# Placing the tables, mask and rotation of the first attention pair in another pool, loading two later pairs block by block, and one result five slots later

## The chip, the cores and the metric

The kernel runs on one core of a Trainium2 chip. The metric is the device time of one execution in microseconds (us); lower is better. PE is the matrix engine, DVE the vector engine, ACT the scalar engine, POOL the GpSimd engine, SP the engine that issues most DMAs.

## The reference

One decoder layer with 512 tokens, width 2048, eight attention heads and eight retention heads of 128, all in float32:

```python
h = rms_norm(x, g_mix)
aq, ak, av, rq, rk, rv, rg = split(h @ w_in)
aq = rotate(rms_norm(aq, q_norm)); ak = rotate(rms_norm(ak, k_norm))   # per head
a_out = block-causal softmax attention(aq, ak, av)                     # 8 heads
r = retention_chunkwise(rotate(rq), rotate(rk) / sqrt(128), rv)        # 8 heads
r_out = silu(rg) * (rms_norm(r) * g_ret)
x = x + concat(a_out, r_out) @ w_o
x = x + (silu(h2 @ w_gate) * (h2 @ w_up)) @ w_down                     # h2 = rms_norm(x)
x = x + (p @ w_ple_proj) * sigmoid(rms_norm(x) @ w_ple_gate + b)
```

With 512 tokens and blocks of 256 the selection of past blocks takes every past block, so attention is plain causal attention.

## The kernel before

**Arithmetic.** Every float32 product is made of three passes. An operand is split (`split`, lines 54 and 55) into a high part, which ACT copies (`wh`, `qkH`, `PH`), and a low part, which DVE subtracts (`wl`, `qkL`, `PL`); `mm3` (line 63) then issues high by high, high by low, low by high. So each weight tile of 128x1024 costs ACT one copy and DVE one subtraction before PE can use it. Transposes go through PE with an identity (line 68, tiles `tp`).

**First stage.** `run(beside)` makes the first projections: the q and k of pair 0 (`Plain`), then four groups by a seven-product scheme: values, the q and k of pairs 1 and 2 (`pairs`), values, and the gates (`gates`, whose silu results `sg` are stored to DRAM, lines 622 and 623; the last of them are made from tiles `e1` and `e5`, printed as `e`). The q and k of pairs 0 to 2 go to DRAM as blocks `zd[i][b]` of 128 rows and are read back as `zr`. The evacuation tiles of the stage lie in a pool `ev` on the right side of SBUF. The stage ends with `ev_ctx.close()`; the pools opened after it may lie on the same bytes, and a tile that does waits until the last access to what lay there is done.

**Mixing stage.** It follows at line 671. Five projections of 32 slots each (pair 3, then four retention pairs) run on PE, and `tick()` counts slots; a slot is six matmuls of 128x512. `at_slot(n, fn)` puts the pieces of attention and retention (turn q and k, scores, softmax, transposed weights, result) between the slots. PE's instructions keep the order in which they are written (`keep_in_program_order`); the order on DVE, ACT, POOL and SP is set when the kernel is built, by a scheduler that simulates the engines. `ATTEND`, `RETAIN` and `MIXED` are the tables of slots; the last entry of a `RETAIN` row is the slot of `result` (transposes of `r`, line 1028), `MIXED[i]` that of `mixed`, which splits a pair's two results into factors, sends them to DRAM (`mix<-o`, line 217) and so precedes the reload `s<-mix` (line 243). From slot 161 on the small projection `pp` runs (line 1115), then the first products of the output projection.

**The code around the change.** `sides` (gains and mask), `cs`, `sn` and the tables `tabs` (printed as `rope`) are loaded and built at lines 751 to 779, in pool `ap`, which is the first pool on the right side. `in_place` rotates one block of `zr`: two products with the sine table into `m` (line 832), one with the cosine table (line 830), one sum (line 81); ACT then scales the k half (line 854). For pair 0 this happens at once, for pairs 1 and 2 at slots 12 to 15 and 27 to 30, behind `load_pair` at slots 6 and 24. `qk_pair` and `p_tiles` give the split q and k and the tiles `PH` and `PL` that hold transposed softmax weights; line 928 sets one strip of `PH` and `PL` to zero, once.

Of the kernel before, what the change touches and what calls it, by code (L numbers as in the profile page):

```python
# [11 lines left out]
F32R = mybir.dt.float32r  # L12
# [5 lines left out]
P = 128  # L18
T = 512
D = 2048  # L20
NB = T // P
# [12 lines left out]
def layer_kernel(ctx, tc, x, xT, pT, g_mix, wqk, w_vg, qk_norm, g_ret, w_ow, g_ffn,  # L34
                 w_gu, w_dn, g_ple, w_pl, b_pg, w_pp,
                 ident_c, rope_c, ropeT_c, decay_c, mask_c, out):
    nc = tc.nc
    PSUM = bass.MemoryType.PSUM

    def pool(name, bufs=1, side="left", **kw):  # L40
        return tc.tile_pool(name=name, bufs=bufs, side=side, reuse_waits="tile", **kw)
# [8 lines left out]

    def split(H, L, src, scale=None):

        if scale is None:
            return (nc.scalar.activation(H, src, AF.Copy),  # L54
                    nc.vector.tensor_tensor(L, src, H.bitcast(F32), op=ALU.subtract))  # L55
        return (nc.scalar.activation(H, src, AF.Copy, scale=scale),
                nc.vector.scalar_tensor_tensor(L, src, scale, H.bitcast(F32),
                                               op0=ALU.mult, op1=ALU.subtract))
# [81 lines left out]
    def paced(ins, by):  # L140
        tc.add_manual_dep(ins.ins, by.ins.name, mybir.DependencyInfo(mybir.DependencyClass.Sync, mybir.DependencyReason.DATA),
                          reason="paced")
# [17 lines left out]
    lead = [None]  # L160
# [32 lines left out]
    def factors(a0, a1, sink):  # L193
# [7 lines left out]
        for p in ORDER:  # L201
            if p in first:
                first[p]()
            H, L, end = sink(p)
            split(H, L, made[p])
            end()
# [350 lines left out]
    zd = [[dram.tile([P, T], F32, name=f"z{i}_{b}") for b in range(NB)] for i in range(3)]  # L557
# [31 lines left out]
    def values(i):  # L589
        def finish(th, nh, b, part, _):  # L590
            tb = 2 * th + b
            H = ev_tile("o", 4, name="vH", dt=F32R)
            L = ev_tile("o", 4, name="vL", dt=F32R)
            split(H, L, part, rstd[0][:, tb:tb + 1])
# [74 lines left out]


    mix_ctx = ctx.enter_context(ExitStack())
    ap = mix_ctx.enter_context(pool("ap", side="right"))
    pools["ev"] = ev2 = mix_ctx.enter_context(pool("ev_mix", side="right"))
    acc_ctx = ctx.enter_context(ExitStack())
# [9 lines left out]
    def at_slot(n, fn):  # L684
        assert n > slot[0]
        pieces.setdefault(n, []).append(fn)
# [41 lines left out]
    def raw_pair():  # L728
        return [rawq.tile([P, 2, T], F32, name="zr", tag="bd") for _ in range(2)]

    def projection(rows):

        accs = [acc_p.tile([P, T], F32, name="acc", tag="acc") for _ in range(4)]
        for u in range(NC // 2):
            wh, wl = weights()
            for f in range(4):
                tick()
                at = slice(f * P, (f + 1) * P)
                for c in range(2):
# [4 lines left out]
                    else:  # L744
# [9 lines left out]
                                    ap=[[0, P], [HD, 2], [1, HD]]))  # L754
# [5 lines left out]
    cs, sn = (ap.tile([P, NB, HD], F32, name=n, tag="pt", bufs=2) for n in ("cs", "sn"))  # L760
    nc.sync.dma_start(cs, rope_c[:, 0])
    nc.sync.dma_start(sn, rope_c[:, 1])
    def load_pair(i, by=None):
        z = raw_pair()
        for b in range(NB):
            ins = nc.sync.dma_start(z[b // 2][:, b % 2], zd[i][b])
            if by is not None:
                paced(ins, by)
        blocks[i] = [z[b // 2][:, b % 2] for b in range(NB)]
        return ins  # L770

    blocks = {}
# [4 lines left out]
            nc.vector.tensor_tensor(tabs[1][:, s, :, here], sn[:, :, here],  # L777
                                    gain[:, s:s + 1, there].to_broadcast([P, NB, 64]), op=ALU.mult)
    rstd1 = rstd[0]
    last_load = load_pair(0)  # L780
    for _ in range(4):
        fetch(last_load)

# [7 lines left out]

    def qk_pair():
        H = ap.tile([P, T], F32R, name="qkH", tag="qkH", bufs=4)
        L = ap.tile([P, T], F32R, name="qkL", tag="qkL", bufs=4)
        return H, L

    def v_of(i):
# [5 lines left out]

    def p_tiles():

        PH = ap.tile([P, 1664], F32R, name="PH", tag="PH")
        PL = ap.tile([P, 1664], F32R, name="PL", tag="PL")
        return PH, PL

    kept_p = []  # L810
# [46 lines left out]
    def in_place(i, b, made, norms):  # L857
        of = blocks[i][b]
        sq = squares(of) if i == 0 else None
        m = rm_tile("m", (P, 2, 2, 2, HD // 2))  # L860
        z = of.rearrange("p (s h d) -> p s h d", s=2, h=2)
        whole, *halves = turn(z, m, of, b)
        for step in halves + [whole]:
            step()
        norms.append(norm(b, sq) if i == 0 else known[i][b])
        made.append(rotated(z, m, norms[b]))

    def qk_attn(i):

        made, norms = [], []  # L870
        if i == 0:
            for b in range(NB):
                in_place(0, b, made, norms)
        elif i < NPAIR - 1:
            at_slot((6, 24)[i - 1], lambda: load_pair(i, lead[0]))
            for b in range(NB):
                at_slot((12, 27)[i - 1] + b, lambda b=b: in_place(i, b, made, norms))
        else:
            got, ins = [], None
            for b, acc in enumerate(projection(True)):  # L880
                z = rp_tile("z", (P, 2, 2, HD))
                m = rm_tile("m", (P, 2, 2, 2, HD // 2))
                got.append((z, m, squares(acc)))
                for step in turn(z, m, acc, b):
                    ins = step()
            with tc.issue_after(ins.ins):
                for b, (z, m, sq) in enumerate(got):
                    norms.append(norm(b, sq))
                    made.append(rotated(z, m, norms[b]))
        return made, norms  # L890
# [151 lines left out]
    def mixed(i, made):  # L1042
# [10 lines left out]
              ((73, four(77), four(81), 89), (83, four(87), four(91), 99)))  # L1053
    RETAIN = (((100, 100, 103, 109, 116), (108, 110, 111, 117, 123)),
# [3 lines left out]
    MIXED = (28, 56, 81, 104, 126, 151, 168, 191)  # L1058

    def heads(i, made):  # L1060

# [304 lines left out]
```

## Time and profile before

| | us |
|---|---|
| median of 3 runs | 2364.56 (2363.38 to 2364.84) |
| profiled execution, its own time | 2362.4 |
| its span | 2360.6 |
| PE busy | 2300.4, 97% |
| DVE busy | 1928.0, 82% |
| ACT busy | 1230.6, 52% |
| mean granted PE clock | 0.991 |

The span is the stretch from the first to the last recorded instruction; the profiled execution's own time has 1.8 us around it. Busy PE time counts matmuls as they overlap, so PE's idle stretches, and the stretches in which the granted clock is half, are what can be won without less work. In a timeline row the bracket holds the idle time of that engine just before the row and what ended it.

### The profile page before, as it was taken

To read this page: it belongs to the slowest core of one execution; us is meant where nothing else is said; L and a number is where in the kernel's file an instruction comes from. 1 tells how busy PE (TensorE), PEld (TensorE's weight loads), DVE (VectorE), ACT (ScalarE), POOL (GpSimd) and SP (SyncE) were. 2 spreads that over 40 slices of the span, in tenths; PEclk is the share of its full clock that TensorE was granted. 3 is DMA by queue.
4 is the path that set the end of the run, shared out by engine and by line. 5 is a ranking of instruction groups with operands and counts; after the bars stand their busy time and mean duration, and the time that the engine had idled before them with its cause. 6 is when DMAs were issued, how large, how long until landed. Compare 5 with 4: busy or idle time off the path is not lost.

```text
span 2360.6 us, 29420 instructions
## 1 busy us (share of the span) xinstructions
PE 2300.4 (97%) x10445; PEld 1896.0 (80%) x10445; DVE 1928.0 (82%) x2601; ACT 1230.6 (52%) x1882; POOL 116.2 (5%) x135
## 2 busy tenths in 40 slices
PE   9999995899999999999999999999999999999999
PEld 7888874788887887888888888888888878888877
DVE  8887876777767897789888988898879887888798
ACT  8645453455555566445544554455445433447644
POOL 0004010000111000000000000000000000000000
PEclk9999997999999999999999999999999999999999
DMA  7635863546676869585457645865595776769863
GB/s 243 239 124 172 267 182 100 154 155 178 217 226 250 325 231 394 155 254 193 153 176 254 205 144 177 251 206 146 194 388 200 248 312 196 274 242 351 299 206 125
DMA packets 183843, 519.72 MB, mean 220 GB/s; under 512 B 20240, under 2 KB 33168, under 8 KB 179600
## 3 DMA queue, kind: packets, MB, share of 16 engines
q1 hardware_dynamic: 169600, 467.50, 55.3%
q0 software_dynamic: 13952, 50.34, 10.1%
q8 instruction: 82, 1.34, 0.2%
q14 instruction: 65, 0.53, 0.1%
q10 hardware_dynamic: 144, 0.01, 0.0%
HBM read 413.95 MB, written 149.95 MB: 239 GB/s over the span
## 4 chain that ended last, share of the span: by engine, by line
PE 53%; DVE 4%; DMA 3%; issue 1%; ACT 0%; SPq 0%; ACTq 0%; DVEq 0%
PE Y L63 23%; PE Z L63 15%; PE X L63 14%; DVE wl L55 2%; DMA raw<-in_w_dn 2%; DVE raw L81 2%; PE tp L68 1%; ACT wh L54 0%; DMA s<-a 0%; DMA raw<-in_w_gu 0%; DMA pp<-pp 0%; DMA xin<-x 0%; DVE e L81 0%; DVE o L55 0%; DVE t L78 0%
## 5 line engine op out<-in xcount | busy, mean ns | idle before, releaser
L54 ACT ACTIVATE wh<-raw 128x1024 fp32r<-128x1024 f32 (+1 forms) x740 | 782.7, 1059 | 873.7 <-PE Y L63 304.8
L55 DVE TENSOR_TENSOR wl<-raw,wh 128x1024 fp32r<-128x1024 f32 (+1 forms) x740 | 900.2, 1219 | 293.5 <-ACT wh L54 292.0
L63 PE MATMUL Y<-wh,s 128*128 128x512 f32 (+1 forms) x1704 | 537.9, 389 | 0.8 <-ACT wh L54 0.8
L81 DVE TENSOR_TENSOR raw<-raw 128x1024 f32<-128x1024 f32 x348 | 419.4, 1218 | 25.1 <-DMA raw<-in_w_vg 10.9
L63 PE MATMUL Z<-wh,s 128*128 128x512 f32 x1212 | 382.4, 389 | 0.2 <-ACT wh L54 0.2
L63 PEld LDWEIGHTS Y<-wh,s 128*128 128x128 f32 x1704 | 319.3, 188 | 66.6 <-ACT wh L54 1.8
L63 PE MATMUL Y<-wl,s 128*128 128x512 f32 x852 | 333.3, 391 | 0.8 <-DVE wl L55 0.7
L63 PE MATMUL X<-wh,s 128*128 128x512 f32 x1008 | 319.1, 390 | 1.7 <-ACT wh L54 1.7
L63 PEld LDWEIGHTS Z<-wh,s 128*128 128x128 f32 x1212 | 227.2, 188 | 46.5 <-ACT wh L54 0.7
L63 PE MATMUL Z<-wl,s 128*128 128x512 f32 (+1 forms) x606 | 238.7, 394 | 2.9 <-DVE wl L55 2.7
L63 PEld LDWEIGHTS X<-wh,s 128*128 128x128 f32 x1008 | 189.1, 188 | 41.4 <-ACT wh L54 2.5
L63 PE MATMUL X<-wl,s 128*128 128x512 f32 x504 | 197.2, 391 | 1.2 <-DVE wl L55 1.2
L63 PEld LDWEIGHTS Y<-wl,s 128*128 128x128 f32 x852 | 160.1, 188 | 35.6 <-DVE wl L55 3.0
L63 PE MATMUL Y<-wh,r 128*128 128x512 f32 x520 | 170.9, 390 | 1.3 <-ACT wh L54 1.1
L63 PE MATMUL acc<-h,wh 128*128 128x512 f32 x512 | 162.0, 398 | 0.0
L63 PEld LDWEIGHTS Z<-wl,s 128*128 128x128 f32 x606 | 113.9, 188 | 28.6 <-DVE wl L55 5.9
L63 PE MATMUL Z<-wh,r 128*128 128x512 f32 x372 | 122.0, 389 | 0.0
L63 PEld LDWEIGHTS Y<-wh,r 128*128 128x128 f32 x520 | 97.4, 188 | 21.9 <-ACT wh L54 2.1
L63 PEld LDWEIGHTS X<-wl,s 128*128 128x128 f32 x504 | 94.7, 188 | 21.6 <-DVE wl L55 2.3
L63 PEld LDWEIGHTS acc<-h,wh 128*128 128x128 f32 x512 | 91.8, 189 | 15.4 <-DVE zr L963 0.3
L63 PE MATMUL Y<-wl,r 128*128 128x512 f32 x260 | 102.4, 394 | 0.5 <-DVE wl L55 0.5
L63 PE MATMUL acc<-h,wl 128*128 128x512 f32 x256 | 100.4, 392 | 0.0
(241 smaller groups left out, 2839.3 us busy)
## 6 DMA issues: line engine op xcount, KB each, us to landing
raw<-in_w_gu SPq DMA_DIRECT2D x172, 512.0 KB, 5.6
raw<-in_w_dn SPq DMA_DIRECT2D x85, 512.0 KB, 6.6
a<-o SPq DMA_DIRECT2D x154, 256.0 KB, 4.9
raw<-in_w_vg SPq DMA_DIRECT2D x64, 512.0 KB, 5.1
s<-a SPq DMA_DIRECT2D x21, 1536.0 KB, 8.6
raw<-in_wqk SPq DMA_DIRECT2D x47, 512.0 KB, 4.9
raw<-in_w_ow SPq DMA_DIRECT2D x32, 512.0 KB, 6.8
xin<-x SPq DMA_DIRECT2D x60, 256.0 KB, 5.9
```

Of the source, the lines that this page charges most:

```text
L54: return (nc.scalar.activation(H, src, AF.Copy), nc.vector.tensor_tensor(L, src, H.bitcast(F32), op=ALU.subtract))
L55: nc.vector.tensor_tensor(L, src, H.bitcast(F32), op=ALU.subtract))
L63: ins = nc.tensor.matmul(*args, **kw)
L68: ins = nc.tensor.transpose(o, a, ident)
L81: nc.vector.tensor_tensor(o, a, b, op=ALU.add)
```

## The change

A new pool `far` is opened before `ap` on the right side, and `qkL`, `PH` and `PL` are taken from it; the tables, `cs`, `sn`, the mask and the rest stay in `ap`, which now begins behind `far`. `load_pair` becomes `load_block`: pairs 1 and 2 (the second and third) are loaded one block at a time, at slots 5, 7, 9, 11 and 17, 19, 21, 23, and each block is rotated three slots after its load. In `RETAIN` the result of the second head of the third retention pair goes from slot 165 to 170, and `MIXED` of that pair from 168 to 171.

```diff
     mix_ctx = ctx.enter_context(ExitStack())
+    far = mix_ctx.enter_context(pool("far", side="right"))
     ap = mix_ctx.enter_context(pool("ap", side="right"))
...
-    def load_pair(i, by=None):
-        z = raw_pair()
-        for b in range(NB):
-            ins = nc.sync.dma_start(z[b // 2][:, b % 2], zd[i][b])
-            if by is not None:
-                paced(ins, by)
-        blocks[i] = [z[b // 2][:, b % 2] for b in range(NB)]
+    def load_block(i, b, by=None):
+        if b == 0:
+            z = raw_pair()
+            blocks[i] = [z[b // 2][:, b % 2] for b in range(NB)]
+        ins = nc.sync.dma_start(blocks[i][b], zd[i][b])
+        if by is not None:
+            paced(ins, by)
         return ins
...
-    last_load = load_pair(0)
+    last_load = [load_block(0, b) for b in range(NB)][-1]
...
-        L = ap.tile([P, T], F32R, name="qkL", tag="qkL", bufs=4)
+        L = far.tile([P, T], F32R, name="qkL", tag="qkL", bufs=4)
...
-        PH = ap.tile([P, 1664], F32R, name="PH", tag="PH")
-        PL = ap.tile([P, 1664], F32R, name="PL", tag="PL")
+        PH = far.tile([P, 1664], F32R, name="PH", tag="PH")
+        PL = far.tile([P, 1664], F32R, name="PL", tag="PL")
...
-            at_slot((6, 24)[i - 1], lambda: load_pair(i, lead[0]))
             for b in range(NB):
-                at_slot((12, 27)[i - 1] + b, lambda b=b: in_place(i, b, made, norms))
+                n = (5, 17)[i - 1] + 2 * b
+                at_slot(n, lambda b=b: load_block(i, b, lead[0]))
+                at_slot(n + 3, lambda b=b: in_place(i, b, made, norms))
...
-              ((142, 142, 145, 151, 158), (150, 152, 153, 159, 165)),
+              ((142, 142, 145, 151, 158), (150, 152, 153, 159, 170)),
...
-    MIXED = (28, 56, 81, 104, 126, 151, 168, 191)
+    MIXED = (28, 56, 81, 104, 126, 151, 171, 191)
```

Three places show what this does to the order in which the engines get their instructions. The first is SP at the end of the first stage; `sg` is the DRAM tensor of gate results, `raw<-in_wqk` a weight tile of the next projection. Before:

```order
L711 DMA raw_3721<-in_wqk 128x1024
L623 DMA sg_150<-e1_2616 128x512
L623 DMA sg_150<-e1_2617 128x512
L711 DMA raw_3864<-in_wqk 128x1024
L753 DMA sides_3043<-in_qk_norm 128x256
L757 DMA sides_3043<-in_mask_c 128x128
L761 DMA cs_3049<-in_rope_c 128x512
L762 DMA sn_3050<-in_rope_c 128x512
```

And now:

```order
L768 DMA zr_3063<-z0_3_189 128x512
L712 DMA raw_3068<-in_wqk 128x1024
L712 DMA raw_3072<-in_wqk 128x1024
L754 DMA sides_3046<-in_qk_norm 128x256
L758 DMA sides_3046<-in_mask_c 128x128
L762 DMA cs_3052<-in_rope_c 128x512
L763 DMA sn_3053<-in_rope_c 128x512
L802 DMA v_3178<-v_0_148 128x2x256 x4
L623 DMA sg_150<-e5_2674 128x512
```

The four table loads, and the loads of `v` behind them, stood behind the last six stores of `sg`; they now stand ahead of all six.

The second place is DVE over the same stretch; `wl` is the low part of a weight tile, `e1<-Y` the evacuation of the stage's last product. Before:

```order
L55 TENSOR_TENSOR wl_3138<-raw_3041,wh_3137 128x1024
L78 TENSOR_TENSOR e1_2616<-Y0_2958,e1_2616 128x512
L78 TENSOR_TENSOR e1_2617<-Y1_2959,e1_2617 128x512
L55 TENSOR_TENSOR wl_3142<-raw_3065,wh_3141 128x1024
L928 TENSOR_SCALAR PH_3246<-ident_72 128x128
L928 TENSOR_SCALAR PL_3247<-ident_72 128x128
L756 TENSOR_SCALAR sides_3043<-sides_3043 128x128
L774 TENSOR_TENSOR rope_3047<-cs_3049,sides_3043 128x512 x2
L777 TENSOR_TENSOR rope_3048<-sn_3050,sides_3043 128x4x64 x4
L832 TENSOR_TENSOR m_3075<-zr_3059,rope_3048 128x4x64
```

And now, where the tables and the eight products into `m` stand further ahead still:

```order
L55 TENSOR_TENSOR wl_2954<-raw_2414,wh_2953 128x1024
L831 TENSOR_TENSOR zr_3062<-zr_3062,rope_3050 128x512 x2
L831 TENSOR_TENSOR zr_3063<-zr_3063,rope_3050 128x512 x2
L55 TENSOR_TENSOR wl_2973<-raw_2437,wh_2972 128x1024
L81 TENSOR_TENSOR zr_3062<-zr_3062,m_3078 128x512
L81 TENSOR_TENSOR zr_3062<-zr_3062,m_3092 128x512
L81 TENSOR_TENSOR zr_3063<-zr_3063,m_3106 128x512
L55 TENSOR_TENSOR wl_3137<-raw_3042,wh_3136 128x1024
L81 TENSOR_TENSOR zr_3063<-zr_3063,m_3120 128x512
L55 TENSOR_TENSOR wl_3141<-raw_3044,wh_3140 128x1024
L78 TENSOR_TENSOR e1_2616<-Y0_2958,e1_2616 128x512
L78 TENSOR_TENSOR e1_2617<-Y1_2959,e1_2617 128x512
```

Tables and rotation of the first pair have moved from behind `e1<-Y` to ahead of it, between the `wl` of the stage's last products; the zero strips of `PH` and `PL` come behind the first `qkL`.

The third place is DVE where the second pair's softmax meets the third pair's rotation, in the projection of the fourth pair; `pt` is a softmax row block, `mx` its maximum, `zr` and `m` the third pair's blocks, `z` and `m` made from `acc` the fourth pair's. Before:

```order
L830 TENSOR_TENSOR zr_3582<-zr_3582,rope_3047 128x512
L832 TENSOR_TENSOR m_3791<-acc_3129,rope_3048 128x4x64 x2
L830 TENSOR_TENSOR z_3797<-acc_3130,rope_3047 128x512
L832 TENSOR_TENSOR m_3798<-acc_3130,rope_3048 128x4x64 x2
L915 TENSOR_SCALAR mx_3738<-mx_3738,ms0_3_1957 128x1
L830 TENSOR_TENSOR z_3804<-acc_3131,rope_3047 128x512
L830 TENSOR_TENSOR zr_3582<-zr_3582,rope_3047 128x512
L919 RECIPROCAL sm_3704<-sm_3704 128x1
L81 TENSOR_TENSOR zr_3582<-zr_3582,m_3746 128x512
L919 RECIPROCAL sm_3742<-sm_3742 128x1
L81 TENSOR_TENSOR zr_3582<-zr_3582,m_3759 128x512
L920 TENSOR_SCALAR pt_3703<-pt_3703,sm_3704 128x384
```

And now:

```order
L917 TENSOR_SCALAR mx_3724<-mx_3724,ms0_2_1948 128x1
L913 TENSOR_TENSOR at_3750<-at_3750,sides_3046 128x128
L55 TENSOR_TENSOR wl_3741<-raw_3738,wh_3740 128x1024
L915 TENSOR_REDUCE mx_3755<-at_3750 128x1
L55 TENSOR_TENSOR PL_3248<-tp_3745,PH_3247 128x2x128
L921 RECIPROCAL sm_3728<-sm_3728 128x1
L831 TENSOR_TENSOR z_3793<-acc_3132,rope_3050 128x512
L833 TENSOR_TENSOR m_3794<-acc_3132,rope_3051 128x4x64 x2
L917 TENSOR_SCALAR mx_3755<-mx_3755,ms0_3_1957 128x1
L922 TENSOR_SCALAR pt_3727<-pt_3727,sm_3728 128x384
```

The third pair's rotation is gone from this stretch (it now stands some 30 to 60 instructions earlier, among the softmax of the first pair's second head), and `pt` of 128x384 has one `z` and one pair of `m` ahead of it where it had three `z` and the whole rest of the rotation. On PE the order of all instructions is the same but for one place: the four transposes of `r` that begin the `result` of the seventh pair's second head stand 30 matmuls, five slots, later.

## Rows read from the trace of the kernel before

**Rows 1.** The page's first section: busy time, share of the span, instructions.

```profile
PE 2300.4 (97%) x10445; PEld 1896.0 (80%) x10445; DVE 1928.0 (82%) x2601; ACT 1230.6 (52%) x1882; POOL 116.2 (5%) x135
```

**Rows 2.** What PE waited for from 340 to 480 us: engine, line and tile, what it waited for, us in total, times, longest.

```profile
PE tp L68 <- DVE zr L81: 17.9, 1, 17.9
PE tp L68 <- DVE pt L920: 10.7, 2, 8.3
PE tp L68 <- DVE PL L55: 3.3, 1, 3.3
PE tp L68 <- DVE qkL L55: 0.9, 1, 0.9
```

**Rows 3.** The same from 690 to 760 us.

```profile
PE tp L68 <- DVE r L1022: 4.7, 2, 3.8
PE at L63 <- DVE PL L55: 1.3, 1, 1.3
```

**Rows 4.** Busy time by engine in the four stretches in which the granted clock is half (stretch, its length, busy time and instructions of PE, weight loads, DVE, ACT, POOL; granted clock; DMA share; GB/s).

```profile
362.80:383.30 20.50, 5.03 (x15) 3.47 (x15) 11.50 (x26) 2.98 (x9) 0.00 (x0) 0.50 0.42 132
407.10:410.60 3.50, 3.50 (x12) 2.80 (x11) 1.26 (x3) 1.74 (x3) 0.00 (x0) 0.51 0.00 0
451.50:461.80 10.30, 5.99 (x20) 5.14 (x21) 7.62 (x19) 5.19 (x11) 0.00 (x0) 0.50 0.06 14
707.50:714.40 6.90, 5.67 (x15) 4.46 (x16) 5.29 (x16) 3.33 (x8) 0.55 (x1) 0.51 1.03 417
```

**Rows 5.** The same columns for three other stretches.

```profile
346.56:361.10 14.54, 13.41 (x60) 10.77 (x58) 7.33 (x7) 7.51 (x9) 3.04 (x3) 1.00 0.62 214
...
420.00:430.00 10.00, 9.15 (x47) 7.45 (x47) 7.51 (x19) 4.67 (x10) 0.87 (x1) 1.00 0.41 112
...
710.00:740.00 30.00, 29.95 (x137) 24.90 (x136) 20.82 (x33) 18.82 (x40) 6.64 (x13) 0.93 1.04 377
```

**Rows 6.** SP's queue in order of time: start, time to issue, DMA, number.

```profile
335.23 6.51 SPq L711 DMA_DIRECT2D raw<-in_wqk  x3
...
361.71 0.94 SPq L623 DMA_DIRECT2D sg<-e  x2
...
363.24 0.41 SPq L753 DMA_DIRECT2D sides<-in_qk_norm  x1
...
364.64 0.42 SPq L762 DMA_DIRECT2D sn<-in_rope_c  x1
...
728.88 1.46 SPq L243 DMA_DIRECT2D s<-mix  x3
```

**Rows 7.** DVE in order of time at the end of the first stage.

```profile
359.53 1.28 DVE L78 TENSOR_TENSOR e<-Y,e 128x512 f32<-128x512 f32 x2
...
363.92 0.23 DVE L928 TENSOR_SCALAR PH<-ident 128x128 fp32r<-128x128 f32 x1 [1.60 <-DMA sg<-e]
...
367.85 0.23 DVE L756 TENSOR_SCALAR sides<-sides 128x128 f32<-128x128 f32 x1 [2.54 <-DMA sides<-in_qk_norm]
```

**Rows 8.** DVE's groups of instructions from 360 to 382 us: busy us, mean ns, idle before.

```profile
L832 DVE TENSOR_TENSOR m<-zr,rope 128x256 f32<-128x256 f32 x8 | 2.8, 416 | 0.0
L830 DVE TENSOR_TENSOR zr<-zr,rope 128x512 f32<-128x512 f32 x4 | 2.5, 680 | 0.0
L81 DVE TENSOR_TENSOR zr<-zr,m 128x512 f32<-128x512 f32 x4 | 2.5, 680 | 0.0
L777 DVE TENSOR_TENSOR rope<-sn,sides 128x256 f32<-128x256 f32 x4 | 1.4, 419 | 0.0
L774 DVE TENSOR_TENSOR rope<-cs,sides 128x512 f32<-128x512 f32 x2 | 1.3, 688 | 1.4 <-DMA cs<-in_rope_c 1.4
```

**Rows 9.** PE in order of time: the first transposes, the first matmul, two later ones three matmuls apart, and the first scores (`at`) of the mixing stage, and a matmul of the output projection.

```profile
377.89 2.28 PE L68 MATMUL tp<-ident,zr 128*128 128x128 f32 x4 [17.92 <-DVE zr L81]
379.83 0.77 PE L63 MATMUL acc<-wh,h 128*128 128x512 f32 x1
...
384.27 0.39 PE L63 MATMUL acc<-wl,h 128*128 128x512 f32 x1
...
384.96 0.39 PE L63 MATMUL acc<-wl,h 128*128 128x512 f32 x1
...
386.09 0.28 PE L63 MATMUL at<-qkH 128*128 128x256 f32 x1
...
740.67 0.40 PE L63 MATMUL X<-wh,s 128*128 128x512 f32 x1
```

**Rows 10.** DVE's groups from 445.3 to 455.4 us, in which PE waits for `pt`.

```profile
L830 DVE TENSOR_TENSOR z<-acc,rope 128x512 f32<-128x512 f32 x3 | 2.0, 678 | 0.0
L81 DVE TENSOR_TENSOR zr<-zr,m 128x512 f32<-128x512 f32 x3 | 2.0, 671 | 0.0
L832 DVE TENSOR_TENSOR m<-zr,rope 128x256 f32<-128x256 f32 x4 | 1.5, 419 | 1.0 <-DMA mix<-o 1.0
...
L830 DVE TENSOR_TENSOR zr<-zr,rope 128x512 f32<-128x512 f32 x2 | 1.4, 676 | 0.0
```

**Rows 11.** From issue to landing of DMAs: of the blocks `zr` from 360 to 440 us (least, median, most); of the tables from 355 to 400 us and of the reload from 700 to 740 us (KB each, median).

```profile
DMA to landing us min/median/max: 2.6/3.5/8.4
...
sn<-in_rope_c SPq DMA_DIRECT2D x1, 256.0 KB, 5.4
...
s<-mix SPq DMA_DIRECT2D x9, 512.0 KB, 8.9
```

## The prediction

> **What bounds the kernel now.** I read the page's busy times first. PE is busy for 97% of the span, DVE for 82%, ACT for 52% [rows 1]: PE sets the time, and less waiting, or less work at half clock, is all that an edit of order can win. Then the view of what PE waited for, over the two stretches that the change touches. From 340 to 480 us there are 32.8 us of waits, all before transposes, all for DVE: 17.9 in one piece, 10.7 in two (8.3 and 2.4), 3.3, 0.9 [rows 2]. From 690 to 760 there are 4.7 for `r` (3.8 and 0.9) and 1.3 for `PL` [rows 3]. [...]
>
> The 17.9 us are explained by two queues. SP issues the last stores of `sg` at 361.71 and the tables only behind them, `sides` at 363.24, `sn` at 364.64 [rows 6]. DVE, whose order is fixed, stands at the zero strip of `PH` until such a store is done, and then waits for `sides` until 367.85 [rows 7]. Only then come tables and rotation, 2.8 + 2.5 + 2.5 + 1.4 + 1.3 us [rows 8] and 0.23 for the gain, 10.7 us in all, and PE's first transposes begin at 377.89 [rows 9].
>
> **The change, part by part.** No instruction is added; the orders of DVE, ACT and SP change.
>
> *Tables and first rotation.* SP now issues the tables behind the second of the three weight loads of its row at 335.23 [rows 6], so about 338 to 340. With the 5.4 us that `sn` took to land [rows 11] they are there at about 345. The `v` loads and six stores of `sg` come behind them; nobody waits for these but the zero strips, which are past the first `qkL` now. The 10.7 us of DVE work come between the `wl` of the stage's last products. There DVE is busy for 7.33 of 14.54 us [rows 5], so it has 7.2 us to spare and 3.5 spill over. Queued behind is `e<-Y`, which ended at 359.53 + 1.28 = 360.8 [rows 7] and would end at 364.3. It empties the banks of the stage's last product, and the mixing stage's accumulators lie where those lay, so PE's first matmul waits for it: 364.4 in place of 379.83 [rows 9], 15.4 us. Of the 3.5 us from 379.83 to 383.3, run at half clock, 1.7 would come back, if the remaining wait of some 4 us (part of it inside the stage, before a `wl`) leaves the clock alone. I take the middle, 16.3. The ends: 20.4 (the whole wait and the whole 2.5 of half clock), and 13.0 (a third of the 7.2 us cannot be filled, and the clock stays low).
>
> On the clock the rows say this: beside the wait of 0.9 us the granted clock stays at 1.00 [rows 5], and behind 3.8 us it is at 0.51 [rows 3, 4]. [...]
>
> *Second pair by blocks, slots 5 to 14.* PE waits here 3.3 + 2.4 us and loses 1.75 to the clock. In the new order two of the four sums of that rotation stand behind the `pt` that PE waits for; that is 2 x 0.68 [rows 8], 1.4. Half of the clock's price may go with it, 0.9. I take 2.3; the ends are 0 (another instruction ends the wait) and 7.5 (all of it).
>
> *Third pair by blocks, slots 17 to 26.* Its rotation moves from 440 to 455 us to about 425, among the softmax of the first pair's second head, where PE waited only 0.9 us. Two pairs of `m` (4 x 0.42) and one `zr` (0.68) [rows 8] now stand ahead of the last `pt`, and behind that in the queue the `qkL` and `PL` that PE's next transposes need: 2.4 us lost. The ends are a gain of 0.9 and a loss of 4.7, two whole blocks at 0.84 + 0.68 + 0.68 each and a little.
>
> What it leaves is the place of the 8.3 us wait. In that stretch DVE spends 2.0 + 1.5 + 1.4 = 4.9 us on the third pair [rows 10], and the `pt` came last. Now one `z` (0.68), two `m` (0.84) and some 0.6 of small rows stand ahead of it: 2.1 us of the wait stay, 6.2 go, and with them the 3.0 of half clock, since 2.1 is nearer to the 0.9 that cost no clock than to the 8.3 that did. I take 9.2; the ends are 4.9 (the rotation's own time, no clock back) and 11.3.
>
> *The late result.* The transposes of `r` move five slots on. Three matmuls take 0.69 us at full clock (384.27 to 384.96, [rows 9]), a slot 1.38, five of them 6.9; the `r` that PE waited 3.8 us for is then there 3 us ahead. So 3.8 go, and the 2.8 of half clock: 6.6. But what comes behind is a reload. From 710 to 740 us the DMA share is 1.04 [rows 5]; the engines have nothing free. `s<-mix`, issued at 728.88 [rows 6], lands 8.9 us later [rows 11], at 737.8, and PE uses the last of it at 740.67 [rows 9]. If PE is 6.6 us earlier, it wants it at 734.1, and waits 3.7. The later 0.9 and 1.3 [rows 3] lie behind DVE work that then has time; half of them goes, 1.1. I take 6.6 - 3.7 + 1.1 = 4.0; the ends are 0 and 8.8.
>
> [...]
>
> The sum is 16.3 + 2.3 - 2.4 + 9.2 + 4.0 = 29.4 us. From the profiled execution's own 2362.4 this gives 2333.0; that execution was 2.2 under the median of the runs, so the time I forecast is 2364.6 - 29.4 = 2335. Nothing past 760 us changes its order in a way that a wait there shows.
>
> **The rivals.** *Only the first wait goes.* The later waits are DVE's, DVE has the same work in a shorter time there, and what it no longer does in one place it does in another; then the other four terms come to about nothing, and the time is 2364.6 - 15.4 = 2349. For it speaks that every wait in [rows 2] is for DVE; against it, that 4.9 us leave the stretch of the longest of them.
>
> *All goes.* Waits and half clock together: 32.8 + 4.7 + 1.3 and 10.1 us, 48.9; the time is 2316. Against it is the 3.5 us that DVE cannot fit in, and the full DMA engines at 710.
>
> *The tables land late.* Were they served only at the stage's end, at 361, the 10.7 us would follow, q and k would be ready at 372 and not at 379.7, and the first term would be 8 instead of 16.3: 2343. The share of 0.62 [rows 5] says that there is room earlier.
>
> *Slower: eight waits for blocks.* Each block's rotation now stands in DVE's queue for a load issued three slots (4.1 us) before, and the softmax of the pair in work stands behind it. The blocks landed in 2.6 to 8.4 us, 3.5 at the median [rows 11]. If all eight took 8.4, DVE would stand 4.3 us each time, 34.4 in all: 5.0 us more than the sum, 2370. It decides from a landing time of 4.1 + 29.4 / 8 = 7.8 us on every block; at the median it costs nothing.
>
> **How the numbers follow.** The forecast 0.60 (its own range 2327 to 2343), only the first wait 0.20, all 0.10, tables late 0.06, slower 0.04. The ends of all the terms add up to 13.2 and 48.9 us, that is 2351 and 2316. The range 2319 to 2351 leaves out the slower case and the upper part of "all", and of the others only mishaps that I have no row for. About 0.2%, 4.7 us, is what a measurement of this kernel can tell from no change. Faster by more: 0.94. Within it: 0.03, for a block wait of about 7 us. Slower: 0.03.
>
> **What would show it.** After the change, PE's first matmul of the mixing stage should begin within 6 us of the stage's last, with DVE's `e<-Y` as its releaser, and `sides` should be used on DVE before 347. A wait for `pt` of about 2 us should be left where 8.3 was, with the granted clock at 1.00 there, and new waits of 2 to 3 us before transposes around 410 us on the new scale. Behind the late result no wait for `r`, but one for a DMA of `s<-mix`, or ACT behind it, near the output projection's first tiles. I am wrong in the large if the first wait keeps more than 8 us, if DVE shows idle time for `zr<-z` of more than 2 us a block, or if the clock is half in the same four stretches.

## The result and the profile after

The changed kernel takes 2337.86 us (median of 4 runs, 2333.67 to 2341.09), the kernel before 2363.97 in the same comparison; the ratio is 0.9889, with a 95% interval of 0.9872 to 0.9906. That is 26.1 us less. The forecast was 29.4 us less and 2335, with a range from 2319 to 2351.

What PE waited for from 340 to 460 us in the trace after, in the columns of [rows 2]:

```profile
PE tp L68 <- DVE pt L922: 5.4, 3, 2.9
PE tp L68 <- DVE mx L917: 1.9, 2, 1.4
PE X L63 <- DVE wl L55: 1.8, 1, 1.8
PE at L63 <- DVE qkL L55: 1.5, 1, 1.5
PE tp L68 <- DVE qkL L55: 1.2, 1, 1.2
```

32.8 us of waits have become 11.8, and no single one is longer than 2.9. The wait of 17.9 for the first pair's `zr` is gone without a rest; in its place stand 1.8 for a `wl` inside the first stage and 1.5 for a `qkL` at the first scores. From 660 to 740 us, in the columns of [rows 3]:

```profile
PE acc L63 <- ACT pp L1117: 2.2, 1, 2.2
PE X L63 <- ACT pp L1117: 1.7, 2, 1.5
PE at L63 <- DVE pt L995: 1.5, 2, 1.0
```

No wait for `r`; the two for ACT's copies of `pp` are new, and that for `pt` was 0.3 before. The stretches at half clock, in the columns of [rows 4]:

```profile
349.40:352.80 3.40, 3.40 (x9) 2.62 (x10) 3.40 (x7) 0.69 (x1) 2.54 (x2) 0.50 0.95 311
390.40:393.80 3.40, 3.40 (x11) 2.71 (x12) 1.94 (x5) 1.66 (x5) 0.00 (x0) 0.50 0.00 0
414.30:417.70 3.40, 3.40 (x12) 2.51 (x11) 3.40 (x9) 0.60 (x1) 0.00 (x0) 0.51 0.86 176
```

In this trace 10.2 us of PE's work at half clock have replaced 20.2. In the second of these stretches products of 128x512 into `acc` begin 0.43 us apart (391.45 to 391.88, 392.73 to 393.16), and 0.23 behind it (394.36 to 394.59). From this I estimate the price of a stretch as half of PE's work in it: 5.1 us where it was 10.1.

The end of the first stage, SP's queue first, then DVE, then PE, each in order of time:

```profile
339.11 0.38 SPq L754 DMA_DIRECT2D sides<-in_qk_norm  x1
...
340.49 0.42 SPq L763 DMA_DIRECT2D sn<-in_rope_c  x1
...
367.34 0.94 SPq L623 DMA_DIRECT2D sg<-e  x2
```

```profile
344.08 0.23 DVE L757 TENSOR_SCALAR sides<-sides 128x128 f32<-128x128 f32 x1
...
364.20 1.29 DVE L78 TENSOR_TENSOR e<-Y,e 128x512 f32<-128x512 f32 x2
...
366.81 0.68 DVE L55 TENSOR_TENSOR qkL<-tp,qkH 128x512 fp32r<-128x512 f32 x1
369.56 0.23 DVE L930 TENSOR_SCALAR PH<-ident 128x128 fp32r<-128x128 f32 x1 [2.07 <-DMA sg<-e]
...
370.73 0.68 DVE L55 TENSOR_TENSOR qkL<-tp,qkH 128x512 fp32r<-128x512 f32 x1
```

```profile
349.22 0.66 PE L63 MATMUL X<-wl,h 128*128 128x512 f32 x1 [1.81 <-DVE wl L55]
...
364.33 0.60 PE L68 MATMUL tp<-ident,zr 128*128 128x128 f32 x4
365.03 0.47 PE L63 MATMUL acc<-wh,h 128*128 128x512 f32 x1
...
371.47 0.39 PE L63 MATMUL at<-qkL,qkH 128*128 128x256 f32 x1 [1.49 <-DVE qkL L55]
```

The tables are issued 28 us before the last stores of `sg` and no longer behind them, `sides` is used at 344.1 where it was 367.9 [rows 7], and PE goes from the stage's last product into the first transposes without a gap. The zero strips of `PH` still wait for a store of `sg`, and a `qkL` is queued behind them.

PE has the same matmuls in the same order in all kernels here but for the four transposes of `r`, so the start of one and the same matmul can be looked up in every trace. Cut at seven of them, the time in us between each and the next is:

| from, to (place in the trace after) | before | after, three traces | saved, mean | predicted |
|---|---|---|---|---|
| 300 to 372: stage's end, to the first scores | 86.9 | 71.8, 71.5, 71.2 | 15.4 | 16.3 |
| 372 to 400: second pair's blocks | 29.5 | 28.3, 28.0, 28.1 | 1.3 | 2.3 |
| 400 to 425: third pair's blocks | 22.3 | 25.1, 25.0, 24.5 | -2.6 | -2.4 |
| 425 to 460: where the third pair was | 43.3 | 34.8, 38.1, 36.2 | 6.9 | 9.2 |
| 460 to 660 | 200.1 | 200.0, 200.1, 200.0 | 0.0 | 0 |
| 660 to 735: late result and reload | 79.1 | 75.5, 75.4, 75.3 | 3.7 | 4.0 |
| sum | 461.2 | 435.4, 438.1, 435.4 | 24.9 | 29.4 |

The second and third trace after are those of the runs e5 and e12 below, and the mean of the three is what the column "saved" is taken from. From 735 to 2300, where nothing was changed, it is 1565.0 before and 1564.6, 1563.3 and 1569.8 after. A row of this table can be read to some tenths where its three values agree, a time of a whole run only to several us; the experiments are therefore read by such stretches first.

### The profile page after: what moved, and what is told of

It reads as the page before. It is cut to its first block, busy times and chain, and to the rows that moved or that the text cites. A ratio compares the mean times of both kernels' runs of the same rounds, so it can differ in the third digit from the quotient of the medians.

```text
span 2335.0 us, 29426 instructions
## 1 busy us (share of the span) xinstructions
PE 2296.6 (98%) x10445; PEld 1891.6 (81%) x10445; DVE 1926.5 (83%) x2601; ACT 1229.3 (53%) x1882; POOL 117.2 (5%) x135
## 3 DMA queue, kind: packets, MB, share of 16 engines
q0 software_dynamic: 13952, 50.34, 10.1%
## 4 chain that ended last, share of the span: by engine, by line
PE 53%; DVE 5%; DMA 3%; issue 1%; ACT 1%; SPq 0%; ACTq 0%; DVEq 0%
PE Y L63 23%; PE Z L63 15%; PE X L63 14%; DMA raw<-in_w_dn 2%; DVE wl L55 2%; DVE raw L81 2%; PE tp L68 1%; ACT wh L54 1%; DMA raw<-in_w_gu 0%; DMA pp<-pp 0%; DMA xin<-x 0%; DVE o L55 0%; DVE e L81 0%; DVE t L78 0%; DVE e L1273 0%
## 5 line engine op out<-in xcount | busy, mean ns | idle before, releaser
L81 DVE TENSOR_TENSOR raw<-raw 128x1024 f32<-128x1024 f32 x348 | 420.9, 1223 | 27.9 <-DMA raw<-in_w_vg 11.2
L63 PEld LDWEIGHTS Z<-wl,s 128*128 128x128 f32 x606 | 113.8, 188 | 27.9 <-DVE wl L55 5.2
```

The lines of the kernel that those rows point to most:

```text
L63: ins = nc.tensor.matmul(*args, **kw)
L81: nc.vector.tensor_tensor(o, a, b, op=ALU.add)
```

## The experiments

**The parts one at a time.** The main question was whether the four places pay each by themselves. Rival: the parts need each other, since DVE has the same work as before and only its order differs.

e1 takes only the pool:

```diff
+    far = mix_ctx.enter_context(pool("far", side="right"))
     ap = mix_ctx.enter_context(pool("ap", side="right"))
...
-        L = ap.tile([P, T], F32R, name="qkL", tag="qkL", bufs=4)
+        L = far.tile([P, T], F32R, name="qkL", tag="qkL", bufs=4)
```

(`PH` and `PL` likewise.)

> Only the pool far is added to the kernel before (qkL, PH, PL taken from it); pair loads and the late result stay as they were. My theory (each part works at its own place): the first term alone, 14 to 16 us, so about 2349; PE's waits for pt around 430 (8 us) and for r around 690 (3.8 us) stay. Rival (the parts need each other): under 10 us or over 20 us. PE's first matmul of the mixing stage within 6 us of the stage's last one in either case.

Measured: 2349.0 us, ratio 0.9936 (0.9914 to 0.9958), 15.9 less than before. From 300 us to the first scores 70.5, against 86.9. The waits for `pt` and `r` stay as they were:

```profile
PE tp L68 <- DVE pt L921: 10.7, 2, 8.9
...
PE acc L63 <- DVE e L78: 1.5, 1, 1.5
...
PE tp L68 <- DVE r L1023: 4.7, 2, 3.8
```

e2 takes only the loads by block and the earlier slots:

```diff
-            at_slot((6, 24)[i - 1], lambda: load_pair(i, lead[0]))
             for b in range(NB):
-                at_slot((12, 27)[i - 1] + b, lambda b=b: in_place(i, b, made, norms))
+                n = (5, 17)[i - 1] + 2 * b
+                at_slot(n, lambda b=b: load_block(i, b, lead[0]))
+                at_slot(n + 3, lambda b=b: in_place(i, b, made, norms))
```

> Only the loads block by block and the earlier rotation of pairs 2 and 3; pools and the late result as before. My theory: 0.9 - 2.3 + 8.2 from the three places as the changed kernel's trace has them, about 7 us with the half clock, so about 2357; the 17.9 us wait stays. Rival (rotation ahead of the softmax only moves the wait): no gain, 2362 to 2367.

Measured: 2356.1 us, ratio 0.9969 (0.9950 to 0.9987), 8.9 less. The three stretches from 372 to 460 us take 26.3, 25.1 and 35.6 us, 8.1 less than before in all; the first wait stays:

```profile
PE tp L68 <- DVE zr L81: 17.8, 1, 17.8
PE tp L68 <- DVE pt L921: 6.1, 3, 3.0
```

e3 takes only the late result:

```diff
-              ((142, 142, 145, 151, 158), (150, 152, 153, 159, 165)),
+              ((142, 142, 145, 151, 158), (150, 152, 153, 159, 170)),
...
-    MIXED = (28, 56, 81, 104, 126, 151, 168, 191)
+    MIXED = (28, 56, 81, 104, 126, 151, 171, 191)
```

> Only the result at slot 170 and the mixing at 171. My theory: the wait for r and its half clock go (6.6 us), a wait of ACT for the stores mix<-o and one for its copies of pp come back (3 us), so 3 to 4 us, about 2360. Rival (reload s<-mix bounds PE in any case): 0 to 1 us, 2363 to 2364.

Measured: 2361.2 us, ratio 0.9989 (0.9975 to 1.0004): 3.8 less by the medians, but the interval holds no change. The last stretch takes 75.6 us against 79.1, 3.5 less, and the new waits are those of the changed kernel:

```profile
PE X L63 <- ACT pp L1115: 2.6, 1, 2.6
PE acc L63 <- ACT pp L1115: 2.2, 1, 2.2
```

The three add up to 28.6 us by the medians; the whole change gave 26.1, 26.9 and 23.6 in its three comparisons. The parts pay each at its own place, and the rival falls. They do not add up to the last us: from 372 to 460 us e2 saves 8.1 and the changed kernel 5.6 at the mean, and e2's trace has one stretch of 3.4 us at half clock there where the other three have two or three.

**Is it the slots or the single loads?** e4 and e11 are one kernel, run twice: the changed one with each pair loaded whole at the first of its slots.

```diff
                 n = (5, 17)[i - 1] + 2 * b
-                at_slot(n, lambda b=b: load_block(i, b, lead[0]))
+                if b == 0:
+                    at_slot(n, lambda: [load_block(i, c, lead[0]) for c in range(NB)])
```

> The changed kernel, but each of the two pairs is loaded whole at slot 5 or 17; the rotations stay at slots 8 to 14 and 20 to 26. My theory: the slots of the rotation do it, not the single loads: within 2 us of the changed kernel, 2336 to 2340. Rival (single loads are needed, since four at once hold up the weight loads behind them in SP's queue or leave DVE waiting for blocks): 4 us or more slower, 2342 and above.

Measured: 2345.9 us, ratio 0.9915 (0.9895 to 0.9935): on the rival's side by the time. But of the 4.7 us between the two traces only 1.2 arose from 300 to 735 us. The kernel was therefore run again beside the changed one, which is e12.

> The kernel of e4 again, beside the changed kernel on one chip. From the traces, 1.2 us of the 8 us between the medians of e4 and the changed kernel arose between 300 and 735 us, the rest behind it, where the two are nearly the same program. Theory: the 8 us were mostly spread between runs; the two medians are now within 4 us. Rival: loading each pair whole really costs 5 us or more, 2343 and above.

> The changed kernel once more, as the yardstick on the same chip for e9, e10 and e11: 2334 to 2342.

Measured: 2342.9 (ratio 0.9916, 0.9895 to 0.9936) against 2339.1 (0.9896, 0.9877 to 0.9914), 3.9 apart. The place repeats: from 400 to 425 us it takes 28.2 us in both traces, against 25.1, 25.0 and 24.5, with a stretch of 6.8 us at half clock in each against one of 3.4 or none. The same transposes wait longer there, first in the trace after, then in e11:

```profile
411.88 0.52 PE L68 MATMUL tp<-ident,pt 128*128 128x128 f32 x3 [0.48 <-DVE mx L917]
```

```profile
415.46 0.77 PE L68 MATMUL tp<-ident,pt 128*128 128x128 f32 x3 [2.62 <-DVE pt L923]
```

Ahead of that `pt` of 128x384 DVE's order in e11 has all eight `m` of the third pair, three of its products with the cosine table and two sums; in the trace after it has four `m`, two products and two sums.

So my theory was too simple. Most of the gain comes from the slots, but the single loads are worth some 3 us at this one place: where the pair is loaded whole, the scheduler puts more of its rotation ahead of the softmax. What they are worth in all is not shown: the intervals of the two ratios overlap, and from 372 to 400 us the two traces of the one kernel differ by 3.4 (27.9 and 31.3, against 28.3, 28.0 and 28.1).

**The yardstick.** e5 is the changed kernel, unaltered.

> The changed kernel itself, once more, beside the next three on one chip, as their yardstick: 2334 to 2341. A theory on the spread of its runs (some 7 us): it comes from waits behind DMAs past 760 us and from half clock stretches that come and go, so inside 340 to 760 us PE's waits should be the same as in its first trace within 0.5 us each.

Measured: 2337.4 us, ratio 0.9887 (0.9868 to 0.9906). The waits were not the same within 0.5 us: 2.36 for `wl` where it was 1.81, and 3.9 for `pt` at 441 us where it was 2.25. In part the spread does come from inside the stretch. The wait for `wl` follows the loads of the tables: DVE builds tables ahead of that `wl`, and stands idle for their DMAs, here in the trace after and in e12:

```profile
345.68 0.69 DVE L775 TENSOR_TENSOR rope<-cs,sides 128x512 f32<-128x512 f32 x1 [0.77 <-DMA cs<-in_rope_c]
```

```profile
346.09 0.23 DVE L757 TENSOR_SCALAR sides<-sides 128x128 f32<-128x128 f32 x1 [1.85 <-DMA sides<-in_qk_norm]
```

With 0.8, 1.3 and 1.9 us of this (trace after, e5, e12) PE waits 1.8, 2.4 and 2.9 for `wl`, each time 1.0 more. Outside of the stretch, the 6.5 us between the three values from 735 to 2300 us are the larger share; e12 has two stretches of 3.4 us at half clock there, the other two have none.

**The zero strips.** In e6 they are ordered behind the second `qkL`.

```diff
+        turned_at = [None]
...
-            split(H, L, tp)
+            turned_at[0] = split(H, L, tp)[1]
...
-                    for t in kept_p:
-                        nc.vector.tensor_scalar(t[:, 1408:1536], ident, 0.0, None, op0=ALU.mult)
+                    with tc.issue_after(turned_at[0].ins):
+                        for t in kept_p:
+                            nc.vector.tensor_scalar(t[:, 1408:1536], ident, 0.0, None, op0=ALU.mult)
```

> The changed kernel, with the zero strips of PH and PL ordered behind the second qkL instead of behind the first. My theory: the 1.5 us wait of the first scores for qkL goes, since the second qkL no longer stands behind the strips, which wait for the last stores of sg: about 1.5 us less in the trace at 372 us, in the time 1 to 2 us. Rival: the mask's sum, which stands behind the strips, becomes late instead and PE waits as long for the first softmax rows around 390 us: 0.

Measured: 2342.1 us, ratio 0.9904 (0.9885 to 0.9924), not faster. The wait of `at` for `qkL` is gone, and 300 to 372 takes 71.0 although the wait for `wl` was 2.7 in this execution; 372 to 400 takes 27.1, without the stretch of 3.4 us at half clock that the changed kernel's three traces have there. Yet the profiled execution was late before all this: the matmul that starts at 300.1 us in the trace after starts at 306.2 here. Its trace shows where: DVE waits 4.4 us for a weight load at 247 us (2.0 in the trace after), PE then waits 2.9 and 1.8 us for `wl`, and 3.4 us at half clock follow. Why the load came late stays open. The step is confirmed where it acts; the time does not show it.

**The late result again.** e7 puts it at 168 and the mixing at 169.

```diff
-              ((142, 142, 145, 151, 158), (150, 152, 153, 159, 170)),
+              ((142, 142, 145, 151, 158), (150, 152, 153, 159, 168)),
...
-    MIXED = (28, 56, 81, 104, 126, 151, 171, 191)
+    MIXED = (28, 56, 81, 104, 126, 151, 169, 191)
```

> The changed kernel with the late result at slot 168 in place of 170 and its mixing at 169 in place of 171. My theory: the new waits of 2.2 and 1.7 us for ACT's copies of pp come from the mixing's splits and stores standing among these copies; two slots earlier the stores mix<-o leave 2.7 us earlier and these waits shrink by 1.5 to 3 us in all, while r is not yet late (at most 0.5 us). Rival (the reload s<-mix and the full DMA engines bound PE there): the waits change their names but not their sum, within 0.5 us.

Measured: 2340.1 us, ratio 0.9897 (0.9883 to 0.9912). What PE waited for from 660 to 765 us:

```profile
PE X L63 <- ACT pp L1117: 2.8, 1, 2.8
PE acc L63 <- ACT pp L1117: 1.6, 1, 1.6
PE at L63 <- DVE pt L995: 0.9, 1, 0.9
```

5.3 us where it was 5.4: the waits changed their size and not their sum, as the rival has it. It is a weak test, though: the stores `mix<-o` left at 696.07 us where they left at 696.56, and not 2.7 us earlier as I had expected. The last stretch of the table takes 76.5, with 3.0 us of PE's work at half clock. Who holds up whom is read from ACT's waits, here of the trace after from 680 to 712 us, and from its DMAs from 676 to 716 us (KB each, median us to landing):

```profile
ACT pp L1117 <- PE acc L63: 3.3, 5, 1.3
ACT wh L54 <- PE acc L63: 3.0, 2, 2.5
ACT pp L1117 <- DMA mix<-o: 2.3, 1, 2.3
```

```profile
mix<-o SPq DMA_DIRECT2D x3, 256.0 KB, 12.4
```

The last tiles of `pp` use the buffers (`o`) from which the mixing's stores `mix<-o` read; these land after 12.4 us, ACT's copy of `pp` waits 2.3 us for them, and PE's next product waits for the bank that this copy empties: that is the wait of `X` (1.5 us at the longest). The wait of `acc` (2.2) comes before it and has another cause. The stores are only just issued then, and ACT has been busy from 689 us with `wh` and the splits of `r`, `o` and `PH`, which its order puts ahead of the copy of `pp` that PE waits for (PE, SP's queue, ACT):

```profile
698.53 0.50 PE L63 MATMUL acc<-wh 128*128 128x512 f32 x1 [2.17 <-ACT pp L1117]
...
696.56 3.20 SPq L217 DMA_DIRECT2D mix<-o  x3
...
697.90 1.06 ACT L1117 ACTIVATE pp<-acc 128x512 f32<-128x512 f32 x2
```

e9 takes traffic away: eight of sixteen stores of `pp` are left out.

```diff
-            nc.gpsimd.dma_start(ppd[b][:, n], t)
+            if n in (0, NS - 1):
+                nc.gpsimd.dma_start(ppd[b][:, n], t)
...
-        nc.sync.dma_start(t[1], ppd[tb][:, s])
+        nc.sync.dma_start(t[1], ppd[tb][:, s // 3 * 3])
```

> The changed kernel without eight of the sixteen stores of pp (column blocks 1 and 2 of the small projection are not stored, and later blocks 0 and 3 are read in their place, so part of the output is another). My theory: behind the late result PE waits because the DMA engines are full from 680 to 715 us, so that mix<-o lands after 12 us and the tiles of pp come free late; with 2 MB less in that stretch mix<-o lands in 8 us or less, and the waits for ACT's copies of pp (2.2 and 1.7 us) fall below 1.5 us in all. Rival (ACT and DVE are simply too busy with the mixing's splits there): these waits stay within 0.7 us.

Measured: 2339.4 us, ratio 0.9895 (0.9876 to 0.9913). What PE waited for from 660 to 765 us, and the stores, of e9:

```profile
PE X L63 <- ACT pp L1117: 4.2, 1, 4.2
...
mix<-o SPq DMA_DIRECT2D x3, 256.0 KB, 9.2
```

They land after 9.2 us, not 8; ACT no longer waits for them. The wait of `acc` is gone too, but by ACT's order, which now has four copies of `pp` between 692 and 698 us among the splits. And `X` now waits 4.2 (to 710.71), since ACT's order has put the squares of `r` (line 1017), which wait for DVE's sum, ahead of the last copies of `pp`:

```profile
707.74 0.31 ACT L1017 ACTIVATE pt<-r 128x128 f32<-128x128 f32 x1 [0.87 <-DVE r L81]
...
708.50 1.08 ACT L1117 ACTIVATE pp<-acc 128x512 f32<-128x512 f32 x2
...
710.06 0.59 ACT L1117 ACTIVATE pp<-acc 128x512 f32<-128x512 f32 x1
```

In sum 4.2 where it was 3.9, so the rival holds by these waits. The last stretch of the table takes 74.6, 0.8 less, although e9 has 2.9 us of PE's work at half clock there and the trace after none; the waits for `pt` (1.5) are gone. So the stores `mix<-o` make one of the waits, and ACT's own order makes the other. The experiment did not empty the DMA engines: their share from 696 to 716 us is 1.04 in e9 as in the trace after, so what the stretch would take beside idle engines stays open.

**How much DVE must fit.** e8 builds the tables on POOL.

```diff
-        nc.vector.tensor_tensor(tabs[0][:, s], cs, gain[:, s:s + 1, :].to_broadcast([P, NB, HD]), op=ALU.mult)
+        nc.gpsimd.tensor_tensor(tabs[0][:, s], cs, gain[:, s:s + 1, :].to_broadcast([P, NB, HD]), op=ALU.mult)
```

(The four products of the sine table likewise.)

> The changed kernel with the six products that build the rotation tables on POOL instead of DVE. DVE is then 2.7 us shorter at the end of the first stage. My theory (the stage's end is bound by the 10.7 us that DVE must fit into 7.2): the wait of 1.8 us for wl at 347 goes, and with it the half clock behind it (1.7 us), and e<-Y is ready 2 to 3 us earlier: 3 to 5 us less by the end of the stage, 2331 to 2335. Rival: POOL takes so long for the six products, or holds up DVE so much beside it, that the rotation starts later than now: no gain, or up to 5 us lost.

Measured: 2339.1 us, ratio 0.9897 (0.9881 to 0.9913), no gain. The wait for `wl` falls to 0.5, but the tables take POOL from 351.1 to 358.5 us where DVE needs 2.7, and DVE stands idle for them:

```profile
351.10 1.31 POOL L775 TENSOR_TENSOR rope<-cs,sides 128x512 f32<-128x512 f32 x1 [19.48 <-DMA cs<-in_rope_c]
352.38 3.53 POOL L778 TENSOR_TENSOR rope<-sn,sides 128x256 f32<-128x256 f32 x2
...
357.89 1.95 DVE L833 TENSOR_TENSOR m<-zr,rope 128x256 f32<-128x256 f32 x4 [2.58 <-POOL rope L778]
```

300 to 372 takes 71.1 us, as the changed kernel does. From 340 to 500 us its granted clock was 1.00 in the mean, and its sum from 300 to 735, 432.6, is the least of all; the time doesn't show that, with 5.2 us lost before 300, behind a late weight load near 247 us as in e6.

e10 leaves work out: the first pair's rotation has no product with the cosine table and no sum, eight instructions of 0.68 us less on DVE.

```diff
-        for step in halves + [whole]:
+        for step in halves + [whole] if i else halves:
             step()
```

(And `plus` in `rotated` is left out for the first pair.)

> The changed kernel, where the first pair's rotation lacks the product with the cosine table and the sum (8 DVE instructions, 5.0 us; the first pair's attention is another then). My theory (at the stage's end DVE must fit 10.7 us into 7.2): 5.7 us fit, so the 3.5 us that spilled over and the waits for e<-Y and qkL go; from 300 us to the first scores 3 to 5 us less than the changed kernel's 71.5 to 71.8, though the wait for wl near 347 stays, since the tables are still built ahead of it. Rival (the wait for e<-Y comes from PE's own late wl and from the order, not from the amount of DVE work): under 1.5 us.

Measured: 300 to 372 takes 68.1 us, 3.4 less than the mean of 71.5, and the wait for `wl` is still there with 1.7. The waits for `e<-Y` and the first scores' wait for `qkL` are gone: DVE's work that did not fit costs the stage's end something. How much is less sure than the 3.4 says, since the changed kernel's traces have longer waits for `wl` or a half clock there. Beside e4 and e11, with the same work, a wait for `wl` of 1.4 and 1.8 and the clock at full, e10 is 1.9 us faster. But the time is 2338.6, ratio 0.9894 (0.9875 to 0.9914), as that of e12: from 372 to 735 it takes 367.6 us where the changed kernel's three traces have 364.8 at the mean, so 2.8 of the 3.4 us are given back. Counted at half the clock takes most of it: in this trace 13.9 us of PE's work from 372 to 735 are at half clock, 7.0 at half, in the other three 6.8 to 9.8, 3.4 to 4.9 at half. One of these stretches, in the columns of [rows 4]:

```profile
384.20:391.00 6.80, 4.61 (x14) 3.25 (x13) 5.97 (x15) 2.80 (x8) 0.00 (x0) 0.50 0.19 72
```

## Why the prediction was right

The prices of half clock in the forecast (2.5, 1.75, 3.0 and 2.8 us, 10.1 in all, and the 1.7 for 3.5 us) are halves of PE's time in the stretches of [rows 4], an estimate; no run shows one of them alone. What the traces show in their place is the 0.43 us between matmuls at half clock against 0.23 at full, and 1.8 us between the trace after and e11 up to the first scores, with one stretch of 3.4 us at half clock and with none.

*Tables and first rotation* (16.3 predicted, 15.4 measured). The mechanism is shown: the pool alone gives it (e1), and DVE's work does spill over (e10), by 1.9 to 3.4 us where I had 3.5. `e<-Y` ends at 364.20 + 1.29 = 365.5, predicted 364.3. Two things in this step were wrong. I had added the whole spill behind `e<-Y`, and named a wait before a `wl` only in passing. In fact 1.8 to 2.9 us are that wait, inside the stage, so that the stage itself ends later and little or 1.5 us of waiting is left for `e<-Y`; and of that wait 0.8 to 1.9 us are not DVE's work but the table loads, for which DVE stands idle. And "nobody waits for these but the zero strips, which are past the first `qkL` now" overlooked what stands behind the strips: the second `qkL`, and 1.5 us of the first scores. In e5 and e12, whose clock stayed up there, PE waited 1.5 us for `e<-Y` instead and not for `qkL`; in e6, with the clock down as in the trace after, neither wait is there, so the turned order does remove it.

*Second pair by blocks* (2.3 and 1.3). The wait for `PL` of 3.3 is gone, but waits for `mx` (1.4) and `pt` (2.9) stand in its place: 4.3 us of waits where there were 5.6, so that the 1.4 of the forecast is right. What did not come is the 0.9 of the clock, since half clock comes behind these waits in all three traces. In e2, where no half clock fell into this stretch, it gave 3.2.

*Third pair by blocks*, the loss (2.4 and 2.6) and the gain behind it (9.2 and 6.9). For the loss the number agrees partly by luck: I had 2.4 us of waits and no clock, and the trace after has 0.9 us more of waits than before (1.7, for `qkL` and `mx`) and a half clock stretch of 3.4 us, 1.7 counted at half. In the gain, the wait left for `pt` was forecast at 2.1 and is 2.25, 3.9 and 2.0 in three traces. The term that was mis-sized is again the clock: I had all 3.0 us of it come back, and in two of the three traces there is a half clock stretch of 3.4 us, again 1.7 by that count.

*The late result* (4.0 and 3.7). The wait for `r` and its half clock went. Of the 3.7 us the clock is 2.8 by the same count; the waits of the stretch fell only from 6.2 to 5.3. That something takes the waits back was right, but the step named the wrong thing, and that the size agrees is luck: PE waits for no reload `s<-mix` there. It waits 1.5 us for the mixing's stores, through the tiles that they hold, 2.2 for ACT's order and 1.5 for DVE's `pt`.

Of the rivals, "only the first wait goes" falls with e2, and with e3 by its stretch, "all goes" with the waits that are left, and "tables late" with `sides` used at 344.1. "Slower: eight waits for blocks" falls with the landing times of the blocks in the trace after, least, median and most; it needed 7.8:

```profile
DMA to landing us min/median/max: 2.6/2.8/3.0
```

## What to carry to other kernels

When a wait hangs on a store that merely shares bytes with the next stage's tiles, as the 17.9 us for `zr` did here, put there what the next stage needs last; then add up what the moved work costs the engine that now does it earlier, against the idle time that this engine has in the very stretch, and look whether the loads for that work land before it is due. In an order that is fixed per engine, look also at what stands one and two places behind a waiting instruction: here the second `qkL` behind the zero strips, 1.5 us. Parts at separate places added up here to 28.6 us, and the whole gave 26.1, 26.9 and 23.6, with more stretches at half clock from 372 to 460 us than e2 had. A gain in front of a stretch with little slack can be given back in it, as 2.8 of 3.4 us in e10's one trace.

## What the runs showed that I had not expected

In these traces the clock does not follow the length of a wait. Behind the wait for `wl` near 347 us the granted clock fell to 0.50 after 1.8 us (trace after) and after 1.9 (e7), and stayed at 1.00 after 2.4 (e5) and 2.9 (e12). All ten traces with that wait say the same: it fell in four (e6 and e9 are the others, after 2.7 and 2.6) and stayed in six, after waits from 1.4 to 2.9. Rows of the two kinds, for the stretch right behind the wait, of e7 and of e12:

```profile
349.90:353.30 3.40, 3.40 (x9) 2.67 (x9) 3.40 (x7) 0.76 (x2) 1.79 (x1) 0.50 0.93 258
```

```profile
350.50:354.00 3.50, 3.46 (x15) 2.88 (x16) 3.50 (x7) 1.32 (x2) 2.77 (x2) 1.00 0.90 258
```

In 3.40 us of work at 0.50 PE has 9 matmuls, in 3.46 at 1.00 it has 15. A half clock stretch can therefore not be promised to go when a wait shrinks to 2 or 3 us; the changed kernel's three traces have two or three of them from 340 to 720 us, and they make part of the spread between the traces. Counted at half each costs 1.7 us; what was measured comes near: from 300 us to the first scores the trace after takes 71.8, with a wait for `wl` of 1.8 and a half clock behind it, and e11, with a wait of 1.8 and none, 70.0. For the 3.0 us that I had all come back behind a wait of about 2 us, a chance of about a half would have been nearer.

Of e8's four table products of 128x256 on POOL two took 1.8 us each (from 352.38 us), while DVE made `wl` (352.35 and 354.10), and two 0.7 (from 357.13), against 0.42 on DVE [rows 8].
